# One core, two transformer blocks: recurrence operands stored as they are loaded, sixteen gate tiles in halves beside the recurrences, attention's loads by the GpSimd queue

## The chip, the core and the metric

The kernel runs on one core of one Trainium2 chip. The metric is the device time of one launch in microseconds (us). The names are those of the profile: PE is the matrix engine (PEld its weight loads), DVE the vector engine, ACT the scalar engine, POOL GpSimd, SP the sync engine, which here only issues DMAs ("SPq" rows). Every engine works through its own instructions in order.

## The reference, cut to what matters

All is float32, 512 tokens, width 1024. A first block (block-sparse attention, pooling, MLP) feeds a second one, whose mixer is where the change lies:

```python
z = xn @ w_in                       # xn: (512, 1024), w_in: (1024, 8000) with all branches' columns
z_r, z_q, z_kc, ..., z_g, z_m = split(z)
y_r = rwkv7_mixer(z_r, ...)         # 16 heads of 64, a recurrence over the tokens:
    # state = state * w_t + (state @ a_t) b_t^T + v_t k_t^T ;  y_t = state @ r_t
y_n = nsa_mixer(z_q, ...)           # 16 heads, three attention branches with a relative bias, 4 groups
gm = sigmoid(z_m).reshape(B, S, 2, D)
merged = gm[:, :, 0] * (y_r @ w_branch_rwkv) + gm[:, :, 1] * (y_n @ w_branch_nsa)
h = h + merged @ w_mix_out          # then cross attention and a convolutional FFN
```

## The kernel before, in words

Activations lie channel by token, 128 channels to a tile. A weight product is made tile by tile of 128 output columns: the weights (128x1024, 512 KB) are loaded into `ws`, ACT rounds them to `wh` (line 221), DVE subtracts to get the rest `wl` (line 222), and PE runs 8 x 3 matmuls of 512 columns (lines 242 to 244: high x high, high x low, low x high). `w_in2` has 59 such tiles: 0 to 26 for the recurrence, 27 to 42 for attention's q, k and compressed inputs, 43 to 58 for the merge gates z_m.

The second block's mixer is built in two stages. In each, Python generators are woven into one program: `weave` takes the stream that has done the least work in proportion to its rate, and a scheduler then orders the instructions of each engine.

- **The projections** (phase `pa1`). Stream "": for each of 8 pairs of heads, three tiles of `w_in2`, and `rwkv_front`, which works out the recurrence's operands and stores them to DRAM (SP queue); `rwkv_solve` inverts triangular blocks on DVE. Stream "_p" (its tiles are `psg_p`): attention's projections, stored to DRAM by the POOL queue, and then six gate tiles, 43 to 48. The rates are 245 and 170.
- **The shared stage** (phase `pa2`). Stream "": `nsa`, the attention of 4 groups of 4 heads, which loads q, k, v and biases from DRAM (SP queue). Stream "_b": `rwkv_backs`, the recurrence, 8 pairs of heads by 8 chunks of 64 tokens, each chunk a chain of small matmuls and DVE copies (lines 873, 887, 890, 896); `rwkv_load` brings the next pair's operands into `L1`, `L4` and `rb` by halves, while `rwkv_operands` readies the rest, among it the product of `KB` with the decays on POOL (line 828). Stream "_m" (tiles `psg_m`): the other ten gate tiles, 49 to 58, with one `ws`, one `wh` and one `wl` buffer, since the second buffers hold the recurrence's `L1`, `L4` and `even`. When "_m" and the recurrence are done, `merge` starts the product with `w_br_r` (tiles `psg_b`) beside what is left of attention, and then that with `w_br_n`. The rates are 190, 240 and 65.

`L1`, `L4` and `rb` come from three DRAM tensors that hold other layouts: `vgd` (rows 6 and 7), `tad` and `trd`. Ten DMAs of 64 KB make one half, and `L1`'s land in runs of 64 floats. `wsplit` and `gemm_g` have a path for weights in halves (`self.halves`), which nothing switches on.

## Time and profile before

| | us |
|---|---|
| median of 3 runs (lowest, highest) | 2106.37 (2103.17, 2115.03) |
| the profiled execution, its own time | 2105.03 |
| its span, first to last instruction | 2103.3 |
| the projections, to the last pair's operands and to the stage's end | 646 to 1031, to 1053 |
| the shared stage, to the recurrence's end and to attention's end | 1053 to 1442, to 1476 |
| the products with w_br_r and w_br_n after it | 1476 to 1550 |

The times of stages are read from where their lines' first and last instructions stand in the trace. Durations of matmuls overlap: one of 512 columns is shown with 0.40 us, and the next starts 0.23 us later.

### The profile page before, as it was taken

What the parts mean: (1) busy time and instruction counts of PE and PEld (TensorE: products, weight loads), DVE (VectorE), ACT (ScalarE), POOL (GpSimd) and SP (SyncE); (2) the same over time, 40 slices, a digit from 0 to 9 for tenths busy, and PEclk for the clock granted to TensorE, in tenths of its full rate; (3) what the DMA queues carried; (4) which work ended last, traced back from release to release, by engine and by line L of the source; (5) the groups of instructions that cost most, each with busy time, mean ns of one, the idle gap of its engine ahead of it and who ended that gap; (6) DMA issues with size and microseconds to landing.
All of it is one profiled execution on the core that took longest, in us unless ns stands there. A gap on an engine that the chain in (4) does not pass through costs nothing.

```text
span 2103.3 us, 27840 instructions
## 1 busy us (share of the span) xinstructions
PE 2013.3 (96%) x9927; PEld 1629.6 (77%) x9927; DVE 1306.4 (62%) x2983; ACT 925.7 (44%) x1778; POOL 80.0 (4%) x139
## 2 busy tenths in 40 slices
PE   8999999999999999899988889999999999999999
PEld 7778888888887778777766677777878878888887
DVE  5785432554464568778578777888566756666422
ACT  4864532442253233234265566877243443333311
POOL 0000000000003201000100100000000000000000
PEclk9999999999999999899988899999999999999999
DMA  4233232333365655565544445445442122232332
GB/s 160 81 90 96 91 97 94 115 107 124 125 204 149 167 157 175 134 157 172 164 121 110 125 129 141 106 132 177 154 149 86 51 78 92 91 100 91 101 108 83
DMA packets 172491, 256.70 MB, mean 122 GB/s; under 512 B 87200, under 2 KB 102768, under 8 KB 172352
## 3 DMA queue, kind: packets, MB, share of 16 engines
q1 hardware_dynamic: 169024, 244.42, 39.8%
q0 software_dynamic: 3328, 10.49, 1.4%
q8 instruction: 79, 1.29, 0.3%
q14 instruction: 60, 0.49, 0.1%
HBM read 205.12 MB, written 45.53 MB: 119 GB/s over the span
## 4 chain that ended last, share of the span: by engine, by line
PE 47%; DVE 5%; ACT 4%; DMA 3%; issue 1%; SPq 1%; DVEq 0%; ACTq 0%
PE psg L242 8%; PE psg L243 8%; PE psg L244 8%; DMA ws<-in_w_in 2%; PE psg_b L242 1%; PE psg_b L243 1%; PE psg_b L244 1%; PE psb L327 1%; PE psg_p L242 1%; PE psg_p L243 1%; PE psg_p L244 1%; PE pso L331 1%; PE psa L743 1%; DVE ys L776 1%; PE pso L332 1%
## 5 line engine op out<-in xcount | busy, mean ns | idle before, releaser
L221 ACT CAST wh<-ws 128x1024 fp32r<-128x1024 f32 (+2 forms) x283 | 291.5, 1031 | 708.0 <-PE psg L243 461.5
L222 DVE TENSOR_TENSOR wl<-ws,wh 128x1024 fp32r<-128x1024 f32 (+2 forms) x283 | 339.9, 1202 | 272.8 <-ACT wh L221 271.7
L242 PE MATMUL psg<-xh,wh 128*128 128x512 f32 x984 | 393.0, 399 | 4.3 <-ACT wh L221 4.3
L244 PE MATMUL psg<-xh,wl 128*128 128x512 f32 x984 | 392.7, 399 | 0.3 <-DVE wl L222 0.3
L243 PE MATMUL psg<-act,wh 128*128 128x512 f32 x912 | 360.2, 395 | 1.1 <-DVE act L165 1.1
L242 PEld LDWEIGHTS psg<-xh,wh 128*128 128x128 f32 x984 | 185.8, 189 | 47.5 <-ACT wh L221 5.1
L244 PEld LDWEIGHTS psg<-xh,wl 128*128 128x128 f32 x984 | 185.9, 189 | 43.0 <-issue 1.5
L243 PEld LDWEIGHTS psg<-act,wh 128*128 128x128 f32 x912 | 171.1, 188 | 41.9 <-DVE act L165 1.5
L242 PE MATMUL psg<-act,wh 128*128 128x512 f32 x496 | 196.1, 397 | 2.8 <-ACT act L164 1.4
L244 PE MATMUL psg<-act,wl 128*128 128x512 f32 x496 | 196.0, 396 | 0.5 <-DVE wl L222 0.5
L243 PE MATMUL psg<-xl,wh 128*128 128x512 f32 x352 | 139.6, 397 | 0.0
L242 PEld LDWEIGHTS psg<-act,wh 128*128 128x128 f32 x496 | 92.8, 187 | 27.3 <-ACT act L164 2.2
L244 PEld LDWEIGHTS psg<-act,wl 128*128 128x128 f32 x496 | 93.0, 187 | 23.8 <-DVE wl L222 1.3
L314 ACT ACTIVATE p<-p,sm 128x128 f32<-128x128 f32 (+3 forms) x160 | 89.6, 561 | 18.6 <-DVE sm L312 17.3
L243 PE MATMUL psg<-x,wh 128*128 128x512 f32 x216 | 88.4, 409 | 0.0
L330 DVE TENSOR_TENSOR pt<-psb,pt 128x512 fp32r<-128x512 f32 (+3 forms) x160 | 75.7, 486 | 13.2 <-ACT pt L329 10.2
L312 DVE CUSTOM_DVE_ANT_0 p<-psa,bias 128x128 f32<-128x128 f32 (+3 forms) x160 | 75.3, 483 | 12.1 <-PE psa L311 6.6
L329 ACT CAST pt<-psb 128x512 fp32r<-128x512 f32 (+3 forms) x160 | 65.5, 425 | 34.5 <-PE psb L327 31.0
L327 PE MATMUL psb<-ident,p 128*128 128x128 f32 x400 | 77.4, 284 | 3.1 <-DVE p L322 1.7
L243 PEld LDWEIGHTS psg<-xl,wh 128*128 128x128 f32 x352 | 66.3, 188 | 14.1
L242 PE MATMUL psg_p<-xh,wh 128*128 128x512 f32 x176 | 73.0, 415 | 0.6 <-ACT f L956 0.6
L243 PE MATMUL psg_p<-x,wh 128*128 128x512 f32 x176 | 72.2, 410 | 0.0
(485 smaller groups left out, 3883.9 us busy)
## 6 DMA issues: line engine op xcount, KB each, us to landing
ws<-in_w_in SPq DMA_DIRECT2D x59, 512.0 KB
ws<-in_w_fup SPq DMA_DIRECT2D x44, 512.0 KB
ws<-in_w_up SPq DMA_DIRECT2D x32, 512.0 KB
ws<-in_w_down SPq DMA_DIRECT2D x32, 512.0 KB
ws<-in_w_fdn SPq DMA_DIRECT2D x16, 512.0 KB
ws<-in_w_qku SPq DMA_DIRECT2D x12, 512.0 KB
ws<-in_w_out SPq DMA_DIRECT2D x8, 512.0 KB
ws<-in_w_cak SPq DMA_DIRECT2D x8, 512.0 KB
```

The lines of the kernel that those rows point to most:

```text
L221: nc.scalar.copy(wh[:, :n], ws[:, :n])
L222: nc.vector.tensor_tensor(wl[:, :n], ws[:, :n], wh[:, :n].bitcast(F32), OP.subtract)
L242: nc.tensor.matmul(p[:, :n], wh[:, s], h[:, :n], start=c + k == 0, stop=False)
L243: nc.tensor.matmul(p[:, :n], wh[:, s], l[:, :n], start=False, stop=False)
L244: nc.tensor.matmul(p[:, :n], wl[:, s], h[:, :n], start=False, stop=last)
L312: nc.vector.tensor_tensor_reduce(pt, ps[:, :w], bias[:, 512 - w:], 1.0, 3e38, OP.add, OP.min, m[:, i:i + 1])
L314: nc.scalar.activation(pt, pt, AF.Exp, bias=m[:, i:i + 1], scale=-1.0, accum_out=s[:, i:i + 1])
L327: nc.tensor.transpose(ps[:, (i - j) * 128:(i - j + 1) * 128], P[i][:, j * 128:j * 128 + 128], self.ident)
L329: nc.scalar.copy(ph[:, :w], ps[:, :w])
L330: nc.vector.tensor_tensor(pl[:, :w], ps[:, :w], ph[:, :w].bitcast(F32), OP.subtract)
L331: nc.tensor.matmul(o[:, j * 128:], V(j), ph[:, :w], start=first and j == 0, stop=False)
L332: nc.tensor.matmul(o[:, j * 128:], V(j), pl[:, :w], start=False, stop=last and j == 3)
```

## The change

What it does, in its parts:

1. Operand layout. `rwkv_front` stores into two new DRAM tensors, `l1d` and `l4d`, which have the layout of `L1` and `L4`; `rwkv_load` then needs 4 DMAs a half in place of 10. The stores of a pair become 20 in place of 14, and `tad` keeps only its lower half.
2. Gate tiles. All sixteen are made in the shared stage, none in the projections. Their weights come in halves of 128x512 (256 KB): `ws`, `wh` and `wl` are each cut into two buffers used in turn.
3. Queues in the shared stage. `self.side` is the POOL queue there: attention's loads and the gate weights go by it. The gates' stores go by SP.
4. The product of `KB` with the decays, and 16 small memsets of `VS`, move from POOL to DVE.
5. The rates become 140 for "_p" and 95 for "_m".

```diff
     def wload(self, src, n):
         ws = self.f("ws", shape=(128, 1024))
-        self.nc.sync.dma_start(ws[:, :n], src)
+        (self.side if self.sx == "_m" else self.nc.sync).dma_start(ws[:, :n], src)
...
         if self.halves:
             self.turn["w"] = 1 - self.turn.get("w", 0)
             ws, wh, wl = (t[:, 512 * self.turn["w"]:512 * self.turn["w"] + n] for t in self.halves)
-            nc.sync.dma_start(ws, src)
+            (self.side if self.sx == "_m" else nc.sync).dma_start(ws, src)
...
-        nc.sync.dma_start(self.vgd[pr, 6:8].rearrange("e p n -> p e n"), AR.rearrange("p e c t -> p e (c t)"))
+        l1 = self.l1d[pr].rearrange("p (c h t) -> p c h t", c=8, h=2)
+        l4 = self.l4d[pr].rearrange("p (h c t) -> p h c t", h=2, c=8)
+        nc.sync.dma_start(self.vgd[pr, 7], AR[:, 1].rearrange("p c t -> p (c t)"))
+        for h in range(2):
+            nc.sync.dma_start(l1[64 * h:64 * h + 64, :, h], AR[64 * h:64 * h + 64, 0])
...
-        nc.sync.dma_start(self.trd[pr], TR.rearrange("p h c t -> p (h c t)"))
-        nc.sync.dma_start(self.tad[pr], TA.rearrange("p h c t -> p (h c t)"))
+        for h in range(2):
+            nc.sync.dma_start(l1[64 - 64 * h:128 - 64 * h, :, h], TA[0:64, h])
+        nc.sync.dma_start(l4[:, 1], TR[:, 1])
+        for e in range(2):
+            nc.sync.dma_start(l4[64 - 64 * e:128 - 64 * e, 0], TR[64 * e:64 * e + 64, 0])
+        nc.sync.dma_start(self.tad[pr], TA[64:128].rearrange("p h c t -> p (h c t)"))
...
         c = slice(4 * half, 4 * half + 4)
-        big = lambda t: t[pr].rearrange("p (h c t) -> p h c t", h=2, c=8)
+        dma(self.L1[:, c], self.l1d[pr].rearrange("p (c h t) -> p c h t", c=8, h=2)[:, c])
+        dma(self.L4[:, :, c], self.l4d[pr].rearrange("p (h c t) -> p h c t", h=2, c=8)[:, :, c])
         for h in range(2):
-            a, o = slice(64 * h, 64 * h + 64), slice(64 - 64 * h, 128 - 64 * h)
-            dma(self.L1[a, c, h], self.vgd[pr, 6][a].rearrange("p (c t) -> p c t", c=8)[:, c])
-            dma(self.L1[o, c, h], big(self.tad)[:64, h, c])
-            dma(self.L4[o, h, c], big(self.trd)[:64, h, c])
-            dma(self.L4[a, h, c], big(self.trd)[64:, h, c])
+            a = slice(64 * h, 64 * h + 64)
             dma(self.rb[a, h, c], self.vgd[pr, 7][a].rearrange("p (c t) -> p c t", c=8)[:, c])
...
-            nc.gpsimd.memset(VS[64 * h:64 * h + 64, 0, h], 0.0)
+            V.memset(VS[64 * h:64 * h + 64, 0, h], 0.0)
         yield 1.0
-        nc.gpsimd.tensor_tensor(KB, KB, self.decay[:, pr][:, :, None].to_broadcast([128, 8, 128]), OP.mult)
+        V.tensor_tensor(KB, KB, self.decay[:, pr][:, :, None].to_broadcast([128, 8, 128]), OP.mult)
...
-            self.nc.gpsimd.dma_start(self.zmd[t - 43], z)
+            (self.nc.sync if self.sx == "_m" else self.nc.gpsimd).dma_start(self.zmd[t - 43], z)
...
-                nc.sync.dma_start(bias, bass.AP(tensor=self.grd.tensor, offset=self.grd.offset + hd * 1280 + 127,
+                self.side.dma_start(bias, bass.AP(tensor=self.grd.tensor, offset=self.grd.offset + hd * 1280 + 127,
...
         while "_m" in live:
             yield None
-        self.mg = []
+        self.mg, self.halves = [], None
...
-                    yield from g.merge_gates(xs, range(43, 49))
-                g.weave(("", g.rwkv_fronts(xs), 245), ("_p", others(), 170))
+                g.weave(("", g.rwkv_fronts(xs), 245), ("_p", others(), 140))
...
+            g.side = nc.gpsimd
...
-                g.weave(("", until("", g.nsa()), 190), ("_b", right(), 240), ("_m", until("_m", g.merge_gates(xs, range(49, 59))), 65))
+                g.halves = g.f("ws", shape=(128, 1024)), g.f("wh", F32R, (128, 1024)), g.f("wl", F32R, (128, 1024))
+                g.weave(("", until("", g.nsa()), 190), ("_b", right(), 240), ("_m", until("_m", g.merge_gates(xs, range(43, 59))), 95))
```

The loads of q, k, v and of the compressed branch's bias change their queue in the same way as `bias`.

How the instructions stand, at two places. First SP's queue in the shared stage of the kernel before, ahead of a gate tile's weights (`ws<-in_w_in`); `yc`, `ne` and `vgb` belong to the recurrence, `ld`, `f` and `bias` to attention:

```order
L822 DMA ne<-tad 32x4x32
L1050 DMA ld_10980<-qd 128x512
L1050 DMA ld_10982<-qd 128x512
L899 DMA vgb_10803<-vgd 128x512
L923 DMA yrd<-y_9671 128x512
L900 DMA vgb_10804<-vgd 128x512
L1052 DMA f_10984<-gfd 128x1x512
L291 DMA ld_10986<-kvd 64x512 x2
L1168 DMA bias_10989<-grd 128x1x512
L208 DMA ws_11198<-in_w_in 128x1024
L820 DMA yc_11377<-ydr 32x4x32
```

And POOL's queue in the changed kernel, at about the same place (`ydr` is the last block solve's store):

```order
L292 DMA ld_10835<-kvd 64x512 x2
L217 DMA ws_8764<-in_w_in 128x512
L1058 DMA f_10833<-gfd 128x1x512
L791 DMA ydr<-ys_9049 1024x1x32 x2
L217 DMA ws_8764<-in_w_in 128x512 x2
L1174 DMA bias_10838<-grd 128x1x512
L217 DMA ws_8764<-in_w_in 128x512 x3
L1122 DMA ld_11377<-vd 128x256 x2
L1174 DMA bias_11103<-grd 128x1x512
L1122 DMA ld_11382<-vd 128x256 x2
L217 DMA ws_8764<-in_w_in 128x512
```

The weights have left the queue that carries the recurrence's many small loads and stand among attention's loads, two halves to a tile.

Second, PE at the end of attention. Before, the matmuls between those of attention (`psa`, `pso`, `psb`) are the first ones of the product with `w_br_r` (`psg_b`):

```order
L310 MATMUL psa_13507<-kst_12756,qst_12743 128x512
L311 MATMUL psa_13507<-kst_12757,qst_12743 128x512
L242 MATMUL psg_b_13774<-kb_13736,wh_13777 128x512
L310 MATMUL psa_13566<-kst_12749,qst_12746 128x128
L311 MATMUL psa_13566<-kst_12750,qst_12746 128x128
L243 MATMUL psg_b_13774<-kb_13736,wh_13777 128x512
L327 MATMUL psb_13473<-ident,p_13425 128x128 x2
L244 MATMUL psg_b_13774<-kb_13736,wl_13778 128x512
```

In the changed kernel gate tiles (`psg_m`) stand there:

```order
L333 MATMUL pso_13448<-pt_13495,vt_11376 128x384
L328 MATMUL psb_13500<-ident,p_13452 128x128 x2
L328 MATMUL psb_13509<-ident,p_13452 128x128
L243 MATMUL psg_m_13621<-xh_4970,wh_8765 128x512
L244 MATMUL psg_m_13621<-x_927_4972,wh_8765 128x512
L245 MATMUL psg_m_13621<-xh_4970,wl_8766 128x512
L332 MATMUL pso_13448<-pt_13503,vt_11376 128x256
L243 MATMUL psg_m_13621<-xh_5009,wh_8765 128x512
L244 MATMUL psg_m_13621<-x_935_5011,wh_8765 128x512
L245 MATMUL psg_m_13621<-xh_5009,wl_8766 128x512
```

Counted over the whole order, in matmuls of 512 columns: before, 26 of `psg_m` stand ahead of attention's first matmul and 214 behind it; now 32 and 352. Of `psg_p`, 144 are gone; 64 stood behind the last pair's operands, now 48 do. Of the 384 of `psg_b`, 45 stood ahead of attention's end, now 4 do.

## Rows read from the trace of the kernel before

**Rows 1.** The page: span, and busy time of PE and DVE.

```profile
span 2103.3 us, 27840 instructions
PE 2013.3 (96%) x9927; PEld 1629.6 (77%) x9927; DVE 1306.4 (62%) x2983; ACT 925.7 (44%) x1778; POOL 80.0 (4%) x139
```

**Rows 2.** Windows, stage by stage: length, busy us (instructions), granted clock, DMA.

```profile
core 0: us, PE busy (x) PEld busy (x) DVE busy (x) ACT busy (x) POOL busy (x), PEclk, DMA share, GB/s
646.00:1031.00 385.00, 363.72 (x1871) 293.08 (x1871) 277.68 (x739) 134.57 (x209) 40.09 (x74) 0.96 0.59 160
1031.00:1053.00 22.00, 20.80 (x88) 16.17 (x86) 2.18 (x3) 4.48 (x8) 3.52 (x9) 1.00 0.51 154
1053.00:1442.00 389.00, 344.02 (x2001) 278.83 (x2001) 300.15 (x1004) 255.31 (x716) 26.11 (x35) 0.93 0.46 128
1442.00:1476.00 34.00, 32.24 (x162) 25.57 (x161) 29.66 (x77) 27.66 (x67) 0.00 (x0) 0.90 0.53 164
1476.00:1550.00 74.00, 74.00 (x321) 59.50 (x320) 36.23 (x44) 14.77 (x15) 0.00 (x0) 1.00 0.47 146
```

**Rows 3.** Timeline of PE, two following matmuls of 512 columns: start, duration.

```profile
1039.76 0.40 PE L243 MATMUL psg_p<-x,wh 128*128 128x512 f32 x1
1039.99 0.40 PE L244 MATMUL psg_p<-xh,wl 128*128 128x512 f32 x1
```

**Rows 4.** The chain that ended last, 1053 to 1445, its longest pieces: start, us.

```profile
1064.32 9.04 DMA bias<-grd
1173.12 9.82 DMA ws<-in_w_in
1215.71 13.31 DMA ws<-in_w_in
1284.54 9.39 DMA ws<-in_w_in
```

**Rows 5.** Windows over these four pieces and what follows the last three.

```profile
1064.32:1073.36 9.04, 7.43 (x26) 5.85 (x26) 3.47 (x5) 1.76 (x3) 0.70 (x1) 0.50 0.48 115
1173.12:1190.00 16.88, 14.18 (x87) 11.18 (x85) 12.98 (x42) 12.57 (x34) 0.97 (x2) 1.00 0.53 158
1215.71:1240.00 24.29, 16.86 (x95) 14.15 (x93) 13.61 (x46) 13.97 (x38) 0.88 (x3) 0.79 0.39 100
1284.54:1300.00 15.46, 11.09 (x64) 9.96 (x63) 10.80 (x31) 7.09 (x18) 2.42 (x2) 0.89 0.71 210
```

**Rows 6.** Timeline of SP: DMA issues ahead of the late loads.

```profile
1060.52 0.43 SPq L820 DMA_DIRECT2D yc<-ydr  x1
...
1064.32 0.55 SPq L1168 DMA_DIRECT2D bias<-grd  x1
...
1214.49 0.59 SPq L291 DMA_DIRECT2D ld<-kvd  x1
1215.12 0.55 SPq L1168 DMA_DIRECT2D bias<-grd  x1
1215.71 0.85 SPq L208 DMA_DIRECT2D ws<-in_w_in  x1
```

**Rows 7.** One tile, zmd: POOL's issues (ns min/median/max) and time to landing.

```profile
L957 POOL DMA_DIRECT2D zmd<-f x16: 539/543/585, 1006.1 to 1441.0; - x16
...
DMA to landing us min/median/max: 2.3/3.9/8.0
```

**Rows 8.** Groups of POOL, 1046 to 1445: busy us, mean ns | idle before.

```profile
L828 POOL TENSOR_TENSOR kb<-kb,decay 128x1024 f32<-128x1024 f32 x8 | 15.7, 1962 | 96.4 <-DMA kb<-kbd 81.5 <-PE pso L331 14.9
```

**Rows 9.** Timeline of DVE: the same operation beside line 828 and without it, and a 128x1024 one.

```profile
1063.29 1.77 DVE L1151 TENSOR_TENSOR sm<-sm,gt 128x16 f32<-128x16 f32 x1
...
1068.28 1.21 DVE L222 TENSOR_TENSOR wl<-ws,wh 128x1024 fp32r<-128x1024 f32 x1
...
1189.43 0.17 DVE L1151 TENSOR_TENSOR sm<-sm,gt 128x16 f32<-128x16 f32 x1
```

More of the change, by code (lines that the diff above doesn't have):

```diff
@@ L44, in __init__ @@
         self.turn, self.pools, self.right, self.halves = {}, [], [], None
+        self.side = tc.nc.sync
     def pool(self, name, bufs, **k):
@@ L290, in k_load @@
         for b in range(2):
-            self.nc.sync.dma_start(t[64 * b:64 * b + 64], k[64 * par:64 * par + 64])
+            self.side.dma_start(t[64 * b:64 * b + 64], k[64 * par:64 * par + 64])
         return t
@@ L821, in rwkv_operands @@
             dma(Y1[r], src[1][:, ch])
-            dma(self.ne[r, :, r], ta[64:96, h, c2::2, 32:])
+            dma(self.ne[r, :, r], ta[:32, h, c2::2, 32:])
         V.transpose(X0, Y0)
         for h in range(2):
-            nc.gpsimd.memset(VS[64 * h:64 * h + 64, 0, h], 0.0)
+            V.memset(VS[64 * h:64 * h + 64, 0, h], 0.0)
         yield 1.0
-        nc.gpsimd.tensor_tensor(KB, KB, self.decay[:, pr][:, :, None].to_broadcast([128, 8, 128]), OP.mult)
+        V.tensor_tensor(KB, KB, self.decay[:, pr][:, :, None].to_broadcast([128, 8, 128]), OP.mult)
         for q in range(2):
@@ L1049, in nsa_loads @@
             qs.append(self.f("ld"))
-            nc.sync.dma_start(qs[i], self.qd[2 * g + i])
+            self.side.dma_start(qs[i], self.qd[2 * g + i])
         cb = self.f("f")
-        nc.sync.dma_start(cb, bass.AP(tensor=self.gfd.tensor, offset=self.gfd.offset + 4 * g * 1056 + 513,
+        self.side.dma_start(cb, bass.AP(tensor=self.gfd.tensor, offset=self.gfd.offset + 4 * g * 1056 + 513,
                                       ap=[[1056, 4], [-16, 32], [1, 512]]))
@@ L1115, in nsa_groups @@
             for t in range(2):
-                nc.sync.dma_start(z[:, t].rearrange("p k d -> p (k d)"), self.vd[gp, 2 * t2 + t])
+                self.side.dma_start(z[:, t].rearrange("p k d -> p (k d)"), self.vd[gp, 2 * t2 + t])
             v = VT[:, 2 * t2:2 * t2 + 2]
@@ L1427, in emit @@
                          grd=(16, 2, 640), adr=(4, 2, 4, 8, 32, 32), ydr=(4, 64, 32, 32), decd=(8, 128, 8), kbd=(8, 128, 1024),
-                         trd=(8, 128, 1024), tad=(8, 128, 1024), vgd=(8, 8, 128, T),
+                         l1d=(8, 128, 1024), l4d=(8, 128, 1024), tad=(8, 64, 1024), vgd=(8, 8, 128, T),
                          kvd=(8, 128, T), qd=(8, 128, T), vd=(2, 4, 128, 256), zmd=(16, 128, T),
@@ L1464, in right @@
                     yield from g.merge(live)
-                g.weave(("", until("", g.nsa()), 190), ("_b", right(), 240), ("_m", until("_m", g.merge_gates(xs, range(49, 59))), 65))
-            g.halves = None
+                g.halves = g.f("ws", shape=(128, 1024)), g.f("wh", F32R, (128, 1024)), g.f("wl", F32R, (128, 1024))
+                g.weave(("", until("", g.nsa()), 190), ("_b", right(), 240), ("_m", until("_m", g.merge_gates(xs, range(43, 59))), 95))
+            g.halves, g.side = None, nc.sync
         g.banks = {"g": "01", "n": "2", "a": "34", "b": "56", "o": "7"}
```

## The prediction, made before the changed kernel ran

> **What bounds the kernel now.** I read the page first: PE is busy for 96% of the span [rows 1]. That share can't tell one stage from another, because durations of matmuls overlap, so I next asked for windows over the stages that the change touches [rows 2]. The timeline gives the real rate: matmuls of 512 columns start 0.23 us apart [rows 3]. In the products after attention 321 matmuls fill 74.00 us, 0.23 us each: there PE is at its peak. The projections come near it: PE is busy 363.7 of 385 us, DVE 277.7 (72%), and the clock is 0.96. The shared stage doesn't: PE is idle for 45 of 389 us, the clock falls to 0.93 (full speed is 2.4 GHz, the only other level 1.2), DVE is busy 300.2 us (77%) and ACT 255.3 (66%). So the projections are bound by PE; the shared stage is bound by the way in which attention, the recurrence's chain of small steps and the gate tiles wait for each other, engines in order.
>
> Then the chain of waits of the shared stage: four DMAs make its longest pieces, the first bias (9.04 us) and the weights of three gate tiles (9.82, 13.31, 9.39 us), together 41.6 us [rows 4]. SP's timeline shows why they are late. Ahead of the bias stand small loads of the recurrence at 0.43 us an issue, and ahead of the weights attention's loads for the next group [rows 6]: the weights are issued when they are already wanted. ACT stands at the rounding, then PE at the tile's matmuls, and everything queued behind those on both engines waits too.
>
> **The change part by part.** The sum is made against the profiled execution, 2105.0 us, which is 1.3 us under the median of the runs shown; its span is 2103.3.
>
> *The projections lose six tiles.* 6 x 24 = 144 matmuls of `psg_p` go. The order puts 32 instead of 26 gate matmuls ahead of attention, so 138 leave this stage: 138 x 0.232 = 32.0 us if PE alone set the pace. Of this, 128 or so leave the woven part and 10 the tail. DVE loses only 6 x 1.2 us [rows 9] of its 277.7, and its share would rise from 72 to 77%; some of PE's stalls then stay where they were. I take four fifths, -25 us; bounds -16 (half, DVE beginning to bind) and -32. The stores of a pair grow from 14 to 20, 48 more issues on SP at 0.43 to 0.6 us [rows 6], 25 us spread over 400; the runs of 64 floats that the loads of `L1` had move to these stores. DMA engines are busy for 0.59 here [rows 2]. I cost them at nothing: the weights are loaded a tile ahead, and that is the cover. If it went, weights would come late as they do in the shared stage, some 10 us each time [rows 4].
>
> *The shared stage gets them.* 138 matmuls come in. By the order, 97 of them (138 more of `psg_m` less the 41 of `psg_b` that are pushed out) stand between attention's and the recurrence's, 22.5 us at PE's peak, and 41 matmuls of the product with `w_br_r` move behind attention's end, where PE is at its peak already: +9.5 us in full. For the 22.5 us there is room: PE's 45 us of idling, and the clock's 0.07 of 389, 27 us at half rate. But ACT and DVE get 6 x (1.0 + 0.6) and 6 x 1.2 us too, on engines at 66 and 77%, and the gaps are short. Half is my choice, +11; bounds 0 and +22.5.
>
> *The late loads.* With two half buffers each for `ws`, `wh` and `wl`, the load of a half waits only for the rounding of the half before the last, and POOL's queue no longer carries the recurrence's loads. What the four waits cost is not their 41.6 us on the chain, since other work went on beside them. I price it by rate: the four stretches with their aftermath are 65.7 us long and hold 272 PE instructions [rows 5], 4.14 per us; the rest of the stage holds 1729 in 323.3 us, 5.35 per us. At that rate the 272 would have taken 50.8 us: 14.8 us lost, the half clock included (0.50 in the first stretch, 0.79 in the third). I take -15; bounds 0 (each wait replaced by another) and -41.6.
>
> The new loads have a price on POOL: 84 issues in this stage (32 halves, 16 biases, 36 of q, k, v and the compressed bias) at 0.54 us [rows 7], 46 us of 390 on an engine that is idle. POOL's stores land after 2.3 to 8.0 us, 3.9 in the middle; loads of the same size I take to do alike.
>
> *At the start* the last q tiles now end the projections; attention's first loads stand on POOL behind their stores. Store and load at 0.54 + 3.9 us each, and 1.3 us of splitting, are some 10 us, of which the 32 gate matmuls cover 7.4: +3.
>
> *The decays' product on DVE.* 8 x 1.2 us, by the 128x1024 operation [rows 9]. Against it stands what POOL's product costs DVE now: it lasts 1.96 us [rows 8], and beside one a product of 16 elements took 1.77 us on DVE that takes 0.17 without [rows 9]. That is up to 1.6 us each time, 12.8 in all, and nothing where DVE had no such work just then: I take 6. The net is some +4 us of DVE work, half of it hidden: +2. But DVE now waits in order for the load of `KB`, for which POOL could wait (81.5 us of idling) at no cost. In the order the product stands a chunk or more behind the transposes that free the buffer, and a chunk takes some 6 us (389 / 64); a load that takes 9 us would leave 3 us each time, up to +15 in all.
>
> *Fewer loads of operands.* 96 issues less on SP, and other small waits with them: -3; bounds 0 and -8. Casts in halves cost ACT and DVE under 0.2 us a half, hidden by their idle time.
>
> Sum: -25 + 11 + 9.5 - 15 + 3 + 2 - 3 = -17.5, so 2105.0 - 17.5 = **2087 us**.
>
> **A rule against the third part.** The chain above shows weights landing 9 to 13 us after issue [rows 4] where SP took 0.43 to 0.85 us for each issue [rows 6]: the queue's own share is the 6 us or so of issues ahead. The Trainium skill, "DMA: Bandwidth & Descriptors", section "Issuing engines are not separate DMA queues", says that DMAs of all issuing engines run on the same 16 DMA engines, and that several issuers save only the time of issuing. By that rule alone the late loads would give back the issues, an estimate of -6 in place of -15, and the time would be 2096. No sum here rests on it: what I count is that the halves are issued earlier.
>
> **The rivals.**
>
> *The shared stage is full.* The tiles cost PE time one for one (+22.5) and other waits take the place of the late loads (-5): -25 + 22.5 + 9.5 - 5 + 2 = +4, 2109 us. For it: DVE at 77% and a recurrence whose chunks of about 6 us follow each other without a break. Against it: PE's 45 us of idling and the clock. Chance 0.22.
>
> *GpSimd's loads come late (the other side).* The order issues halves in bursts of up to three or four. If POOL's issue or landing is slower than the rows show, each half stops ACT and PE as the three tiles do now. 28 halves are loaded inside the stage; the gain of 17.5 us is gone at 0.6 us for each, and at 1.5 us each the time is 2087 + 42 = 2129. Against it: POOL's issues took 539 to 585 ns, the same all through, in a stage where DVE is busy for 77%, and landed within 8 us [rows 7], against some 13 us between two halves (390 / 30). Those were stores, and one at a time. Chance 0.12. The Trainium skill, "SBUF — State Buffer", section "SBUF: two separate sides", states such a mechanism: GpSimd writes its descriptors through a port pair that some DVE operations hold, and DMAs issued from GpSimd then starve. The sixteen even issues do not show it.
>
> *The changed stage gains more.* Waits go as the chain has them (-41.6 + some replaced, -30) and the tiles fill idle time only (+5): 2087 - 15 - 6 = 2066. Chance 0.2.
>
> The forecast itself, 2075 to 2095, has 0.46.
>
> **How the numbers follow.** A change of this kernel under about 0.5% (10.5 us, the runs span 0.6%) can't be told from none. Faster by more, under 2094.5 us: most of the forecast (0.43) and the rival of a greater gain (0.2), 0.63. Within 0.5%: the rest of the forecast, most of the full stage (0.17) and a little of the late loads, 0.23. Slower: 0.14. The range from 2057 to 2114 leaves out the late loads and the far end of both bounds; the forecast's own is 2075 to 2095.
>
> **What would show it.** Right: the last pair's operands some 22 to 28 us earlier; no weights or bias among the longest pieces of the chain in the shared stage; its clock nearer 1 and its length, to attention's end, from 5 us shorter to 5 us longer than 423 us; the tail behind it longer by about 9 us. Wrong: ACT waiting for `ws` from POOL's queue in many small waits, POOL's issues over 0.6 us, DVE waiting for `KB`, or projections that keep their 385 us.

## The result, and the profile after

The changed kernel takes **2125.66 us** (median of 5 runs, 2123.30 to 2129.51), 19.3 us more than before; the ratio is 1.0082, 95% interval 1.0056 to 1.0109. Measured once more beside other kernels it was 1.0078 (1.0055 to 1.0100). The prediction, 2087 us with "slower" at 0.14, was wrong, and its range (2057 to 2114) did not hold the time.

The page after, the two rows that answer to [rows 1]:

```profile
span 2125.0 us, 27862 instructions
PE 2026.5 (95%) x9927; PEld 1639.4 (77%) x9927; DVE 1319.3 (62%) x3023; ACT 927.0 (44%) x1794; POOL 107.6 (5%) x183
```

Neither says where the time went: as many matmuls, a span 21.7 us longer. The windows after do. The stages begin and end at other times now, so these are cut at attention's first matmul and at its last (columns as in [rows 2]):

```profile
646.00:1060.00 414.00, 372.56 (x1826) 297.49 (x1825) 286.35 (x745) 133.01 (x212) 48.27 (x84) 0.91 0.58 149
1060.00:1482.00 422.00, 385.58 (x2232) 313.92 (x2231) 330.24 (x1109) 284.66 (x797) 48.44 (x79) 0.94 0.47 130
1482.00:1569.00 87.00, 87.00 (x377) 69.99 (x376) 40.83 (x50) 20.14 (x22) 0.00 (x0) 1.00 0.55 172
```

Cut in the same way, the kernel before takes to 1054.5 us, then 419.2 us of attention, then 79.6 us to the last matmul of `psg_b`. After, it takes to 1059.7, then 422.5, then 91.0. So the sum's three pieces came out at +5.2, +3.3 and +11.4 us where the prediction had -22, -5 and +9.5. PE has some 138 matmuls fewer in the first stage and the stage still isn't shorter: the clock there is 0.91, where it was 0.96 [rows 2].

**The end of the projections.** The last pair's operands (VectorE's last write of `lt`) come at 1020 us in the trace, 11 us before the old time (in three other runs with the same projections, `a0_after_again`, `e3_sync` and `e5_kb_pool`, at 1014 to 1018, 14 to 17 us before). But from the last pair to attention's first matmul there are now 40 us, in all four, and there were 23. POOL's timeline after shows what stands there (start, duration, [idle before]):

```profile
1025.48 0.55 POOL L949 DMA_DIRECT2D qd<-f  x1 [5.50 <-DVE f L1040]
1033.68 0.55 POOL L949 DMA_DIRECT2D qd<-f  x1 [7.65 <-DVE f L1040]
1042.12 0.54 POOL L949 DMA_DIRECT2D qd<-f  x1 [7.89 <-DVE f L1040]
1049.79 0.54 POOL L949 DMA_DIRECT2D qd<-f  x1 [7.13 <-DVE f L1040]
1050.58 1.14 POOL L1056 DMA_DIRECT2D ld<-qd  x2 [0.24 <-issue]
```

The last four q tiles are stored 8.1 us apart ((1049.79 - 1025.48) / 3), though 24 matmuls take 5.6 us. Each tile ends in its norm (`head_norm`: ScalarE, PE, a row of small VectorE operations, PE, ScalarE, VectorE). For the last tile this chain stands bare. PE's timeline has its last product, and then the norm's two steps on PE:

```profile
1041.60 0.40 PE L245 MATMUL psg_p<-xh,wl 128*128 128x512 f32 x1
1042.68 1.05 PE L561 MATMUL psn_p<-blk,f 128*128 128x2 f32 x8 [0.69 <-ACT f L1037]
1046.92 1.12 PE L573 MATMUL psn_p<-ident,cx 128*128 128x128 f32 x4 [3.18 <-ACT cx L570]
```

From that product to the tile's store pass 8.2 us (1041.60 to 1049.79), and from the store to attention's first matmul 9.9 more, for the store, the load that is issued straight behind it and the splitting. Not all of the 8.1 us between the stores is such a chain: the last two tiles' 48 matmuls run from 1026.2 to 1041.8 us, 15.6 us in place of 11.1. Matmuls of the norms stand between them, and the first twelve start 0.43 us apart, where 0.23 is the pace at the full clock:

```profile
1028.04 0.63 PE L244 MATMUL psg_p<-x,wh 128*128 128x512 f32 x1
1028.47 0.63 PE L245 MATMUL psg_p<-xh,wl 128*128 128x512 f32 x1
```

Windows of 20 us after show PE's side of it:

```profile
1000.00:1020.00 20.00, 12.27 (x53) 10.48 (x52) 18.41 (x37) 4.85 (x7) 2.76 (x4) 0.67 0.48 136
1020.00:1040.00 20.00, 17.72 (x70) 13.27 (x69) 6.35 (x30) 3.62 (x6) 1.09 (x2) 0.72 0.51 150
1040.00:1060.00 20.00, 14.27 (x61) 10.77 (x60) 8.13 (x25) 7.14 (x14) 6.16 (x11) 0.83 0.43 100
```

and before, the first two of the same stretches, in which the gate tiles still ran:

```profile
1000.00:1020.00 20.00, 16.80 (x65) 12.55 (x64) 17.73 (x46) 6.55 (x10) 2.70 (x4) 0.83 0.59 153
1020.00:1040.00 20.00, 20.00 (x102) 15.80 (x101) 11.62 (x19) 4.78 (x7) 1.65 (x3) 1.00 0.67 218
```

First VectorE is the full engine (18.41 of 20 us, for the last fronts) and PE idles (12.27 busy), and the clock falls to 0.67; then come the q chains, at a clock of 0.72, between the two levels of 2.4 GHz (1.00) and 1.2 GHz.

**The shared stage.** Its chain of waits after, the longest pieces (start, us), answers to [rows 4]:

```profile
1136.29 11.91 DMA ws<-in_w_in
...
1216.85 7.29 DMA yc<-ydr
...
1273.07 7.68 DMA wh<-l4d
...
1435.28 7.38 DMA ws<-in_w_br_r
```

One late gate weight is left of three, the bias is gone, and other loads stand in their place. Why that one was late, POOL's timeline says:

```profile
1135.43 0.80 POOL L1174 DMA_DIRECT2D bias<-grd  x1 [24.78 <-DVE sm L313]
1136.29 0.58 POOL L217 DMA_DIRECT2D ws<-in_w_in  x1
```

and ScalarE's and PE's, behind it:

```profile
1148.23 0.62 ACT L222 CAST wh<-ws 128x512 fp32r<-128x512 f32 x1 [7.75 <-DMA ws<-in_w_in]
```

```profile
1149.17 0.58 PE L332 MATMUL pso<-pt,vt 128*128 128x256 f32 x1 [7.03 <-ACT pt L330]
```

A bias stood 24.78 us at the head of POOL's queue, for a buffer that attention still read (line 313, whose row names `sm`), and the half of weights behind it was issued when the bias was. ScalarE then stood 7.75 us at the rounding, and PE 7.03 us at attention's matmul behind that. The queue is a new one, but still one in order. POOL's issues of weights themselves were as the prediction took them, which answers to [rows 7]; `ws` after, its 28 halves (ns, then landing in us):

```profile
L217 POOL DMA_DIRECT2D ws<-in_w_in x28: 548/557/589, 1071.5 to 1460.4; - x28
...
DMA to landing us min/median/max: 2.5/4.0/11.9
```

The 16 biases took longer to issue there, 802 to 863 ns each, over the 0.6 us that the prediction named as a sign of being wrong; at some 0.25 us more for each it is 4 us of POOL in all.

### The profile page after: what moved, and what is told of

Same layout as the page of the kernel before. It is cut to its first block, busy times and chain, and to the rows that moved or that the text cites. A ratio compares the mean times of both kernels' runs of the same rounds, so it can differ in the third digit from the quotient of the medians.

```text
span 2125.0 us, 27862 instructions
## 1 busy us (share of the span) xinstructions
PE 2026.5 (95%) x9927; PEld 1639.4 (77%) x9927; DVE 1319.3 (62%) x3023; ACT 927.0 (44%) x1794; POOL 107.6 (5%) x183
## 5 line engine op out<-in xcount | busy, mean ns | idle before, releaser
L785 DVE TENSOR_TENSOR ys<-as,ys 128x2 f32<-128x2 f32 (+30 forms) x124 | 60.7, 489 | 1.7 <-DMA ys<-in_y 0.2
L243 PE MATMUL psg_m<-xh,wh 128*128 128x512 f32 x128 | 55.9, 437 | 5.5 <-ACT f L962 4.7
```

Source lines behind the costliest of these rows:

```text
L243: nc.tensor.matmul(p[:, :n], wh[:, s], h[:, :n], start=c + k == 0, stop=False)
L785: V.tensor_tensor(q, a, Y[:, :n, :t + 1], OP.mult)
```

## The experiments

All times are medians; each ratio stands against the kernel before on the same chip, with its 95% interval. Attention's start and end and the end of the products with `w_br_r` and `w_br_n` (`psg_b`) are read from the profile of each kernel (us). One profile is good to some 4 us in such a time: seven kernels with the same order of projections (the q tiles ahead of the v tiles, no gate tiles) begin attention at 1034.6 to 1042.5, and a profiled execution lies up to 6 us from its kernel's median (`e5_kb_pool`, 2112.6 against 2106.5). `a0_after_again` is the changed kernel once more. The kernels ran on several chips, where the kernel before took 2106.1 to 2110.1; differences of medians in the text come out within some 2 us of those between the ratios, but for `e10_thirteen` and `e12_no_loads`, where both are given. "Tiles" says how many gate tiles stand in the shared stage.

| run | tiles | `KB` product | time | ratio | attention starts | its length | to the end of `psg_b` |
|---|---|---|---|---|---|---|---|
| before | 10 | POOL | 2106.4 | 1 | 1054.5 | 419.2 | 79.6 |
| after | 16 | DVE | 2125.7 | 1.0082 (1.0056-1.0109) | 1059.7 | 422.5 | 91.0 |
| a0_after_again | 16 | DVE | 2122.6 | 1.0078 (1.0055-1.0100) | 1056.0 | 422.7 | 91.0 |
| e1_gates_back | 10 | DVE | 2093.1 | 0.9934 (0.9909-0.9959) | 1064.1 | 391.3 | 82.9 |
| e2_v_last | 16 | DVE | 2107.5 | 1.0002 (0.9984-1.0020) | 1039.1 | 426.4 | 93.4 |
| e8_e1_v_last | 10 | DVE | 2084.8 | 0.9897 (0.9873-0.9921) | 1054.1 | 394.8 | 82.8 |
| e3_sync | 16 | DVE | 2133.1 | 1.0125 (1.0095-1.0156) | 1057.2 | 431.8 | 91.0 |
| e4_layout | 10 | POOL | 2108.3 | 1.0014 (0.9996-1.0032) | 1061.6 | 412.5 | 82.9 |
| e7_halves | 10 | POOL | 2117.3 | 1.0035 (1.0021-1.0049) | 1056.5 | 431.4 | 79.3 |
| e9_queue_halves | 10 | POOL | 2097.7 | 0.9945 (0.9926-0.9965) | 1054.8 | 406.9 | 79.3 |
| e5_kb_pool | 16 | POOL | 2106.5 | 0.9993 (0.9979-1.0008) | 1054.5 | 413.9 | 90.8 |
| e6_kb_dve | 10 | DVE | 2101.3 | 0.9964 (0.9951-0.9977) | 1057.0 | 412.0 | 82.9 |
| e13_v_last_kb_pool | 16 | POOL | 2094.8 | 0.9940 (0.9921-0.9959) | 1041.8 | 410.3 | 90.8 |
| e16_best_kb_pool | 10 | POOL | 2096.7 | 0.9945 (0.9928-0.9963) | 1053.3 | 410.0 | 79.5 |
| e10_thirteen | 13 | DVE | 2105.7 | 0.9974 (0.9959-0.9988) | 1059.7 | 414.1 | 84.0 |
| e11_few_matmuls | 16 | DVE | 2101.0 | 0.9965 (0.9948-0.9982) | 1042.5 | 429.1 | 79.8 |
| e12_no_loads | 16 | DVE | 2107.1 | 0.9982 (0.9964-1.0000) | 1036.0 | 420.3 | 93.6 |
| e14_empty | 16 | DVE | 2092.4 | 0.9926 (0.9904-0.9949) | 1042.0 | 409.9 | 82.9 |
| e15_early | 16 | DVE | 2098.1 | 0.9955 (0.9941-0.9970) | 1034.6 | 425.1 | 83.8 |
| e17_pool_early | 16 | POOL | 2087.1 | 0.9895 (0.9870-0.9920) | 1037.4 | 407.2 | 83.9 |

### The end of the projections

Theory T1: the gate tiles were PE work beside the last fronts and q chains, so without them attention starts no earlier. First, six tiles back:

```diff
                     yield from g.projections(xs)
+                    yield from g.merge_gates(xs, range(43, 49))
-                g.weave(("", g.rwkv_fronts(xs), 245), ("_p", others(), 140))
+                g.weave(("", g.rwkv_fronts(xs), 245), ("_p", others(), 170))
...
-                ... ("_m", until("_m", g.merge_gates(xs, range(43, 59))), 95))
+                ... ("_m", until("_m", g.merge_gates(xs, range(49, 59))), 65))
```

> The changed kernel with the first six gate tiles back in the projections; the other ten stay in the shared stage in halves, and the layout, the GpSimd loads and the products on VectorE stay. Theory T1 (the gate tiles were the PE work that filled the end of the projections, which are bound there by VectorE and by the norm chains of the q tiles): the last pair ends at 1025 to 1035 us, attention begins within 3 us of 1054.5, the shared stage is shorter than 422 us by 10 to 20 and the tail by 10; the time is 2095 to 2108, 18 to 30 us under the changed kernel. Rival T2 (GpSimd's loads cost the time) and T4 (the operands' stores cost it): the time stays within 8 us of the changed kernel, 2118 to 2130, since both are still there.

2093.1 us, 32.6 under the changed kernel and 0.66% under the one before: a little better than T1 had it. T2 and T4 fall as the main cause, since GpSimd's loads and the operands' stores are still in. But attention did not start earlier, it started at 1064.1, where T1 had 1054.5: the gain is all in the shared stage (31 us, where T1 had 10 to 20) and behind it (8). So the time came near T1's by another way, and T1 itself is tried by the next run. Its windows:

```profile
646.00:1064.00 418.00, 393.07 (x1969) 315.31 (x1967) 285.41 (x750) 141.31 (x223) 48.73 (x90) 0.95 0.63 158
1064.00:1455.00 391.00, 355.20 (x2127) 293.62 (x2127) 323.81 (x1097) 276.31 (x783) 41.94 (x68) 0.95 0.50 136
```

Then the other order of the projections, q tiles ahead of v tiles, with all sixteen tiles in the shared stage:

```diff
         yield from self.gemm_g(W, range(39, 43), xs, normed)
+        yield from self.gemm_g(W, range(27, 35), xs, normed)
         for gp in range(2):
...
-        yield from self.gemm_g(W, range(27, 35), xs, normed)
```

> The changed kernel with the q tiles ahead of the v tiles, so that the projections end on tiles without a norm chain. T1: attention's first matmul comes 8 to 14 us earlier than 1059.7, and the time falls by as much, to 2111 to 2118. T2 and T4: no change beyond 5 us, 2120 to 2130. If attention starts earlier but its end does not move, the shared stage is bound by something else than its start.

2107.5, 18.2 us under the changed kernel; attention starts at 1039.1, 20.6 us earlier than after, both more than T1 had. POOL's timeline, where the last stores and attention's first load now stand:

```profile
1025.95 2.17 POOL L956 DMA_DIRECT2D vd<-f  x4 [8.46 <-ACT f L955]
...
1031.60 1.12 POOL L1056 DMA_DIRECT2D ld<-qd  x2 [0.23 <-DMA kb<-kbd]
```

The v tiles end in a copy and no norm, and the load follows 5.7 us behind the start of their stores. So the exposed q chains cost some 18 us of the loss: the mean of attention's start is 17.8 us apart, too, between the four profiles with q last (1054.5 to 1059.7) and the seven with v last. Both edits together:

> The changed kernel with six gate tiles back in the projections and the q tiles ahead of the v tiles: ten tiles in the shared stage. T1: the gate tiles already cover the q tiles' chains in the run with the gates back, so putting v behind gives 0 to 8 us, 2085 to 2094. Rival (the end of the projections is bound by VectorE's work for the fronts alone): no change, 2090 to 2096.

2084.8, the fastest of all, just past the good end of T1: the q chains cost 8 us even beside six gate tiles. It beats the kernel before by 1.03% (0.79 to 1.27).

### The layout and the queue

The loads back on SP's queue, the gates' stores on POOL's, otherwise the changed kernel:

```diff
-            g.side = nc.gpsimd
...
-            (self.nc.sync if self.sx == "_m" else self.nc.gpsimd).dma_start(self.zmd[t - 43], z)
+            self.nc.gpsimd.dma_start(self.zmd[t - 43], z)
```

> The changed kernel with the loads of attention, its biases and the gate halves back on SP's queue, and the gate tiles' stores back on GpSimd's. T1: the queue is worth little to either side; the time is 2120 to 2145, the late bias and weights of the kernel before come back and the stage is as long or up to 20 us longer. Rival T2 (GpSimd's loads land late or stand behind its stores): the time falls by more than 10 us, to 2115 or less, most of it at attention's start (23 instead of 40 us from the last pair to the first matmul).

2133.1: T2 falls, POOL's queue is worth 7.5 us (9 between the ratios); the move of the gates' stores to SP is counted in. The layout alone, in the kernel before:

```diff
-        nc.sync.dma_start(self.vgd[pr, 6:8].rearrange("e p n -> p e n"), AR.rearrange("p e c t -> p e (c t)"))
+        nc.sync.dma_start(self.vgd[pr, 7], AR[:, 1].rearrange("p c t -> p (c t)"))
+        for h in range(2):
+            nc.sync.dma_start(l1[64 * h:64 * h + 64, :, h], AR[64 * h:64 * h + 64, 0])
...
```

> The kernel before with the operands' layout alone: L1 and L4 stored as they are loaded, 20 stores a pair instead of 14, 12 loads fewer. T1: within 6 us of the kernel before, 2100 to 2112. Rival T4 (the stores with short runs slow the projections): the last pair ends 8 us or more after 1031, and the time is 2114 or more. As the prediction had it, -3: 2103.

2108.3, no difference in the total. But it is two: attention starts 7 us later, as T4 had it, and its stage is 7 us shorter, as the fewer loads should have it. The prediction had 0 and -3. The later start isn't scatter alone: the two profiles with these stores, six tiles in the projections and q last (`e4_layout`, `e1_gates_back`) start attention at 1061.6 and 1064.1, the four without the stores (`before`, `e6_kb_dve`, `e7_halves`, `e9_queue_halves`) at 1054.5 to 1057.0. Which wait it comes from stays open.

### The late loads

Halves alone, and halves with POOL's queue (the gates' stores then go by SP), both in the kernel before with its ten tiles:

```diff
+                g.halves = g.f("ws", shape=(128, 1024)), g.f("wh", F32R, (128, 1024)), g.f("wl", F32R, (128, 1024))
...
```

> The kernel before with halves for its ten gate tiles, all on SP's queue. If the late weights are cured by the buffers alone, the shared stage loses 8 to 15 us and the time is 2091 to 2098. If they are late because of what stands ahead of them in SP's queue, the time stays within 5 us of before, 2101 to 2110.

```diff
+            g.side = nc.gpsimd
...
+                g.halves = g.f("ws", shape=(128, 1024)), g.f("wh", F32R, (128, 1024)), g.f("wl", F32R, (128, 1024))
...
```

> The kernel before with the GpSimd queue for attention's and the gate tiles' loads, and halves for its ten gate tiles; the layout, the product on GpSimd and the six tiles in the projections stay as before. T1 with the late loads as the shared stage's gain: attention starts at 1054 us as before, the stage is 395 to 405 us instead of 419, and the time is 2085 to 2095. If the layout is what shortened the stage in the run with the gates back (391 us), the stage stays at 410 or more and the time at 2100 or more.

Halves alone cost 0.35%: 2117.3, outside both expectations. The stage grew by 12 us; the chain of waits of that run, its longest pieces, has biases where the weights were, and ScalarE still waits for gate weights, 11.1 us in 3 times:

```profile
1188.80 13.86 DMA bias<-grd
...
1235.97 8.73 DMA bias<-grd
...
1286.78 8.93 DMA bias<-grd
```

With the queue the stage is 406.9 us, 12.3 under before, and ScalarE's wait for gate weights, 12.2 us in 3 times before, is gone; the time is 2097.7, a little above what T1 had. So it takes the queue to cure the late weights (the queue without halves was not tried), and the prediction's -15 is right within 3 us while ten tiles stand there. The first bias is not cured: it stands in this run's chain with 12.07 us, where [rows 4] has 9.04. The Trainium skill, "DMA: Bandwidth & Descriptors", section "Issuing engines are not separate DMA queues", says that more issuing engines save only the time that issuing takes. Half of that is seen: a bias on POOL's queue lands after 9.2 us in the median of the 16 in the profile after, no sooner than the 9.04 us of [rows 4]. The other half isn't: the queue gave 24.5 us of stage (431.4 to 406.9), more than issues of half a microsecond. What stands ahead in a queue waits, too, as the 24.78 us of the bias above show on the other queue; that this is the whole of the 24.5 us is not shown.

### The decays' product

Back on GpSimd in the changed kernel (also the clearing of `VS`), and the reverse in the kernel before:

```diff
-        V.tensor_tensor(KB, KB, self.decay[:, pr][:, :, None].to_broadcast([128, 8, 128]), OP.mult)
+        nc.gpsimd.tensor_tensor(KB, KB, self.decay[:, pr][:, :, None].to_broadcast([128, 8, 128]), OP.mult)
```

> The changed kernel with the decays' product and the clearing of VS back on GpSimd. The prediction's own term: VectorE loses some 4 us of work and its wait for KB, so the time is 0 to 4 us under the changed kernel's 2125, 2121 to 2126. Rival T3 (the product on VectorE is what cost the time): 8 us or more under it, 2117 or less.

> The kernel before with the decays' product and the clearing of VS on VectorE. The prediction's term: +2 us, 2104 to 2112. T3: 8 us or more slower, 2114 or more.

The two don't agree. In the changed kernel GpSimd's product gives 19.2 us (2106.5); in the kernel before VectorE's gives 7 (2101.3). One price of the product can't have two signs. Two more, the same edit in the kernels with v last, of sixteen and of ten tiles:

> The changed kernel once more, beside the three others of this set. All theories: 2120 to 2131. If it comes at 2115 or less, the difference of 19 us between it and the kernel with the decays' product back on GpSimd is not to be trusted.

> The kernel with the q tiles ahead of the v tiles (2107.5 us), with the decays' product back on GpSimd. T3 (the product on VectorE costs some 19 us where sixteen tiles stand in the shared stage): 2085 to 2095. Rival T7 (the product itself is worth little, and what it moved was the order of the stage's other work, which falls out by luck): within 8 us of 2107.5, 2100 to 2115.

> The ten-tile kernel with the q tiles ahead of the v tiles (2084.8 us), with the decays' product back on GpSimd. If the product on VectorE costs what it cost beside sixteen tiles (12 to 19 us), 2065 to 2073. If it costs only where the shared stage holds sixteen tiles, as the kernel before has it (there it gave 7 us on VectorE), 2080 to 2095.

The changed kernel repeats (2122.6). With sixteen tiles GpSimd's product gives 12.7 us again (2094.8), outside T7's "within 8 us"; but the order alone is worth 9.4 us in a run below, so one such pair could still be luck. A third pair of sixteen tiles (`e15_early` and `e17_pool_early`, below) has 11.0. With ten it takes 12 (2096.7, over both expectations). So all five pairs agree in sign: VectorE's product is the better beside ten tiles, GpSimd's beside sixteen. What GpSimd's product does in the ten-tile kernel is in the trace. POOL's product, its idle time before it:

```profile
L834 POOL TENSOR_TENSOR kb<-kb,decay x8: 1887/1890/2307, 1058.9 to 1330.4; 128x1024 f32<-128x1024 f32 x8
its engine sat idle before it (us, times) until:
  DMA kb<-kbd: 36.4, 5
```

and the queue's timeline there:

```profile
1182.19 2.31 POOL L834 TENSOR_TENSOR kb<-kb,decay 128x1024 f32<-128x1024 f32 x1 [7.28 <-DMA kb<-kbd]
...
1204.96 0.83 POOL L1174 DMA_DIRECT2D bias<-grd  x1 [18.86 <-DVE pt L331]
1205.78 0.59 POOL L217 DMA_DIRECT2D ws<-in_w_in  x1
```

On POOL the product waits for `KB` in the queue that now carries attention's loads; before, it waited 81.5 us there [rows 8] with no load behind it. And again a bias waits, as it seems for its buffer, and a gate weight stands behind it: the chain of waits has 18.84 us there and then 8.47 for that weight. In the sixteen-tile runs POOL's product waits only 2.8, 9.8 and 13.7 us for `KB`. On VectorE the sixteen-tile runs are slow in the recurrence itself: from the first product to the eighth there are 294.5 us in the repeated changed kernel and 268.1 with the product on GpSimd, and with v last 280.2 and 263.1. Part of that is the product's own place: on VectorE it starts up to 52 us after `KB` has landed. From attention's first matmul to the recurrence's last store (`yrd`) there are 394.2 us against 385.7, and with v last 396.4 against 382.0. That VectorE waits for `KB` is not seen (0.3 us, one time). What it is in VectorE's order that delays the recurrence there stays open.

### What a gate tile costs in the shared stage

All four with v last. Thirteen tiles there and three in the projections:

```diff
+                    yield from g.merge_gates(xs, range(43, 46))
...
+                ... ("_m", until("_m", g.merge_gates(xs, range(46, 59))), 80))
```

> Thirteen gate tiles in the shared stage, three in the projections, the q tiles ahead of the v tiles. If each tile in the shared stage costs its full 5.6 us of matmuls there and as much is won in the projections, the time lies between the ten-tile kernel of this set and the sixteen-tile kernel with v last (2107.5), within 4 us of their middle, some 2097 to 2101. If the stage has room for some tiles and is full only behind them, the time is at or under that of ten tiles, 2085 to 2093.

2105.7: near sixteen (5.9 us under it between the ratios), not in the middle, outside both expectations. Then the work of the last six tiles, taken out by halves and whole:

```diff
+                    few = self.sx == "_m" and t > 52
+                    nc.tensor.matmul(p[:, :n], wh[:, s], h[:, :n], start=c + k == 0, stop=few and last)
+                    if few:
+                        continue
```

> The kernel with the q tiles ahead of the v tiles (2107.5 us), in which the last six gate tiles of the shared stage leave out two of their three products: 96 matmuls of 512 columns fewer, 22.3 us at the pace of 0.232 us; their loads, casts, subtractions and stores stay. Theory T5 (the shared stage is full on PE, so a tile costs its matmuls one for one): the time falls by 17 to 24 us, to 2084 to 2091. Rival T6 (a tile costs by its loads, casts and places in the order of ScalarE and VectorE): by under 8 us, 2100 or more.

```diff
+                if self.sx != "_m" or t < 53:
+                    wh, wl = self.wsplit(W[t][:, (k0 + c) * 128:(k0 + c + kc) * 128], kc * 128)
```

> The same kernel, in which the last six gate tiles of the shared stage take the weights that stand in the half buffers: their 12 loads, 12 casts on ScalarE and 12 subtractions on VectorE are left out, and all matmuls stay. T5 (full on PE): the time falls by under 6 us, 2101 or more. T6: by 10 us or more, to 2097 or less.

> The kernel with the q tiles ahead of the v tiles, in which the last six gate tiles of the shared stage are left out but for two matmuls, the Tanh and the store: 132 matmuls (30.6 us at 0.232 us) and 12 loads, casts and subtractions fewer. If the tiles' matmuls are paid for one for one by PE: 2074 to 2082. If a tile's work counts by about a third, as the two runs that left out one half of it each had it (6.5 and 0.4 us): 2095 to 2103.

96 matmuls less (22.3 us) give 6.5 us; 12 loads, casts and subtractions less give 0.4 (4.2 between the ratios); both, with 36 matmuls more left out, give 15.1 (30.6 us of matmuls). T5 falls by the first run and T6 by the second: neither part is the whole price, and a tile left out gives back about half of its matmuls' time. Each of these runs has another order, too, and order alone moves 9 us (next section), so the split between the parts isn't shown. The windows of the run without the tiles' work:

```profile
646.00:1042.00 396.00, 366.01 (x1826) 291.83 (x1824) 280.88 (x745) 132.38 (x212) 49.44 (x86) 0.93 0.60 155
1042.00:1452.00 410.00, 368.67 (x2140) 301.10 (x2141) 324.80 (x1098) 279.65 (x789) 40.59 (x66) 0.93 0.48 133
```

It has the work of ten tiles in the stage and yet takes 410 us, where the ten-tile kernel that starts 12 us later takes 395: they end within 3 us of each other. A stage that starts earlier is not over earlier by as much.

### The order alone

The same sixteen tiles with v last, with another share for the gate tiles in the order, and the same with the product on GpSimd:

```diff
-                ... ("_m", until("_m", g.merge_gates(xs, range(43, 59))), 95))
+                ... ("_m", until("_m", g.merge_gates(xs, range(43, 59))), 110))
```

> The kernel with the q tiles ahead of the v tiles, with the number that sets the gate tiles' share of the order at 110 instead of 95: the same instructions in another order in the shared stage. T7: the time moves by 5 us or more to either side of 2107.5, with no work added or taken away. If the order doesn't matter: 2105 to 2110.

> Sixteen tiles, the q tiles ahead of the v tiles, the product on GpSimd and the gate tiles' share at 110. If the two single gains over 2107.5 us (12.7 for the product, 9.4 for the share) are causes of their own they add: 2082 to 2089. If both are ways of one order to fall out better, they don't: 2092 to 2102.

9.4 us for a number that adds and removes no instruction (2098.1), 9.6 us in the profile behind attention, where fewer matmuls of `psg_b` are left. The last product of the gate tiles shows why, first with 95, then with 110 (from 1030 us on: count, ns of one, start of the first and of the last):

```profile
L245 PE MATMUL psg_m<-xh,wl x120: 388/399/796, 1030.9 to 1469.6; 128*128 128x512 f32 x120
L245 PE MATMUL psg_m<-xh,wl x116: 387/397/792, 1041.2 to 1439.3; 128*128 128x512 f32 x116
```

`merge` starts when the gate tiles and the recurrence are done. With 95 the gate tiles last until 4 us behind attention's last matmul (1465.3), with 110 they are over 20 us ahead of it (1459.4). The changed kernel has the first of the two: its last gate matmul ends at 1484.1, 2 us behind attention. With the product on GpSimd 2087.1: the two gains add (20.4 of 22.1 us), as two causes would, and they lie in two places: the product shortens attention's stage (426.4 to 410.3, 425.1 to 407.2), the share what is behind it (93.4 to 83.8, 90.8 to 83.9). This kernel has all sixteen tiles in the shared stage, equals the best one with ten (2084.8) within its spread, and beats both kernels of the case, 0.9895 (0.9870 to 0.9920). Its stage:

```profile
1040.00:1450.00 410.00, 383.44 (x2285) 310.89 (x2284) 328.99 (x1093) 290.13 (x802) 64.09 (x98) 0.98 0.51 141
```

The clock is 0.98 there, against 0.94 after and 0.93 in [rows 2], with the tiles' matmuls in it.

## Why the prediction was wrong

**The step that failed first** is "At the start ... +3". The prediction took the way from the last q tile to attention's first matmul as a store, a load and a splitting, "some 10 us, of which the 32 gate matmuls cover 7.4". These three did take 9.9 us. What it left out is the norm chain in front of the store, 8.2 us for the last tile, and that the last two q tiles, now behind the last pair, run with no gate tile beside them. From the last pair to attention there are 40 us in place of 23, +17 where the prediction's terms make about +1 (the 3 us, less the 10 matmuls that leave the tail). The gate tiles had been the work beside those chains. Putting v behind them gives 18.2 us back.

The term "The projections lose six tiles ... -25 us" itself held up to the last pair: with the operands' stores in both, it comes at 1038.6 and 1040.3 us with six gate tiles in the projections (`e4_layout`, `e1_gates_back`) and at 1014.4 to 1019.9 without them, 22 us earlier in the mean. Attention's start came out at +5 us (+1.5 in the repeated run) where -22 was forecast, 24 to 27 of the 39 us missed; 16 of them are the chains, 7 the stores below. With the q tiles first, six tiles are worth 15 us of attention's start in all (1054.1 to 1039.1), the prediction's bound for "DVE beginning to bind". There (`e2_v_last`) VectorE is nearly full ahead of the last pair, 19.79 of 20 us:

```profile
981.00:1001.00 20.00, 18.19 (x102) 14.50 (x101) 19.79 (x56) 8.86 (x15) 3.48 (x7) 0.89 0.69 116
```

**The layout's stores, "I cost them at nothing".** They cost 7 us of the projections (1061.6 against 1054.5); the fewer loads give 7 back in place of 3. Both were mis-sized, their sum by 3 us, so that it comes out near is luck.

**The shared stage, +11 - 15 + 2 - 3 = -5,** came out at +3.3. The loads' term is right where ten tiles stand (-12.3), with the queue and the halves together; the prediction named the halves first, and alone they cost 12 us of stage. The tiles' term failed: sixteen instead of ten cost 32 us of stage (394.8 to 426.4, v last, VectorE's product; 31 with q last) where the far bound was 22.5. That hangs on the product: with it on GpSimd the two lengths are 410.3 and 410.0, so there the tiles cost the stage nothing, and in the whole times, 2094.8 and 2096.7, the earlier start of 11.5 us pays for a tail that is 11.3 us longer. "+2" for the product was therefore the second mis-sized term: 11 to 19 us beside sixteen tiles, and -7 or -12 beside ten. The prediction priced it by its work on VectorE and feared its wait for `KB`; that wait was not there.

**The tail, +9.5,** is right: +11.4 us.

**The rivals.** "The shared stage is full" names a place that did cost time, but not the cause: leaving out 30.6 us of its matmuls gave 15.1. No rival named the largest loss, that at the end of the projections. "GpSimd's loads come late" came true once, 11.9 us for one half. Its issue was not slow (548 to 589 ns for the halves, though the biases took over 800), and the halves landed after 4.0 us in the middle; a bias ahead of it had waited for a buffer. The Trainium skill, "SBUF — State Buffer", section "SBUF: two separate sides", has GpSimd's descriptors starved by VectorE; these issues do not show it either, in a stage where VectorE is busy for 78%. A third bias buffer, or the biases behind the weights in the queue, would try that cause by itself; it wasn't tried. Nor was the move of the gates' stores to SP's queue, ahead of the recurrence's loads: in the changed kernel SP stands 44 us in all for ScalarE before these stores. But the fastest kernel with sixteen tiles (`e17_pool_early`) has 47 us of it, so the times do not follow it.

**What is shown and what isn't.** Shown by edits: the exposed q chains (18 us with sixteen tiles, 8 with ten), the 7 us of the stores, the queue's cure of the late weights, the two signs of the product, and 9 us from order alone. Read from traces only: that a bias holds back the weights, and that late gate tiles lengthen the tail. Open: why the product on VectorE slows the recurrence beside sixteen tiles. Every edit also changes the order in which the scheduler places the other work, and single differences under some 10 us may be that.

## What to carry to other kernels

Before moving work out of a stage because PE seems to be its bound, look at what is left at the stage's end: work without dependences that is moved away may have been the cover of chains that now stand bare, and putting chain-free tiles last gave 18 us back here without any work added. A second DMA queue can help where a queue in order holds everything behind a load that waits for its buffer, and it can do the same harm itself; look for the longest idle time on the queue's engine and for what is issued right behind it. In a stage of three interleaved streams, price a moved operation by several orders, since moving the product to GpSimd cost 7 and 12 us and gave 11, 13 and 19 us here. Where one stream must be over before the next can start, look at when it ends: a rate of 110 in place of 95 was worth 9 us.

## What was not expected of the hardware

Single profiles of programs that are the same up to a point differed by up to 8 us at that point (1034.6 to 1042.5 at attention's start, seven runs), although medians of a kernel repeated within 3 us (2125.7 and 2122.6). A difference of a few microseconds between two stages of two single profiles says nothing by itself.
